# When the next pair's operands are given to the planner, and the order of GpSimd's sums

## The chip, the cores and the metric

The kernel runs on one core of a Trainium2 chip. The metric is device time in microseconds (us); less is better. The program is a single launch with float32 inputs and outputs.

## The reference

One layer of a decoder trunk for 1024 positions of width 1024: a token mixer (a gated delta rule beside a Conformer convolution), a cross-attention into 256 memory tokens, and a gated MLP with a short convolution between its two projections. Only the MLP's first half matters here:

```python
def conv_glu_ffn(h, w_up, conv_w, conv_b, w_down):     # h 1024 x 1024, w_up 1024 x 5632
    u = causal_dwconv(h @ w_up, conv_w) + conv_b       # width 3
    a, b = jnp.split(u, 2, axis=-1)
    return (jax.nn.silu(a) * b) @ w_down               # w_down 2816 x 1024
```

## The kernel before, in words

The 5632 columns of `w_up` are 44 blocks of 128. Block j of the first 22 and block j + 22 belong together (one is the gate, the other what it gates), so the up projection goes by pairs, j = 0 to 21. Pairs 0 and 1 are plain products. From `PLAIN` = 2 on, a pair is done by `strassen_pair` with seven half products instead of eight: the two weight blocks, each cut into two halves of K = 512, make the 2 x 2 operands A11, A12 (block j) and A21, A22 (block j + 22); the activations, cut by K and by position, make B11 to B22 and four combinations T1 to T4, which are made once ahead of the pairs.

`up_operands(j)` (L1171 to 1191) makes a pair's weights. It loads the two blocks on SyncE's queue (L1175; tile `raw_up`, two buffers in all), has GpSimd form S1 = A21 + A22, S2 = S1 - A11, S3 = A11 - A21 and S4 = A12 - S2 (L1183), and splits A11, S2, S1, S3, A12, S4 and A22 each into a rounded high part (ScalarE, L1188) and the rest (VectorE, L1189). The splits go into four slots of the tag `w`: (A11, S2), (S1, S3), (A12, S4) and (A22). A slot is free for the next pair when the previous pair's products from it are done. One buffer of `raw_up` is free when everything that reads it is done, the last of which is the split of A22 for the second block.

A half product is 12 matmuls (`mm3`, L242 to 244: high by high, high by low, low by high, for four slices of K) into one PSUM bank of 128 x 512. The order in `strassen_pair` is: A11 B11 into bank 0, S2 T2 into bank 1, S1 T1 into bank 2, S3 T3 into bank 3, then A12 B21 on top of bank 0, S4 B22 on top of bank 2, A22 T4 on top of bank 3. Before the last three, the first results must have been read out: L1204 (ScalarE) copies bank 0 to `p1`, L1206 (VectorE) adds bank 1 to it, L1208 makes `u3` = bank 2 + `p1`, L1210 makes a part of `ub` = bank 3 + `u3`. L1212, L1214 and L1216 read the final banks. Then `conv3` (L1157 ScalarE, L1159 VectorE twice for each block) and `gate_mid` (L1164 ScalarE, L1165 VectorE, store on ScalarE's queue, L1166) finish the pair beside the next pair's products.

What order the engines' queues have is not written out by hand: the Tile framework's planner goes through the program with a cost model of its own, and of what it takes as ready on an engine it puts first what the program gave it first. Every engine then works its queue in that fixed order and waits by semaphores. Before the change `up_operands(j + 1)` is called ahead of `strassen_pair(j)`, so all of the next pair's loads, sums and splits rank ahead of all of pair j's own work. `tc.keep_in_program_order(ins)` pins an instruction behind the one that the program gave the same engine before it; that is an order in the queue and no wait.

After the pairs the down projection (`down_operands`, `step_mm`) follows, with loads of `w_down` (`rbM`) and of the stored results (`ma`).

Of the kernel before, what the change touches and what calls it, by code (L numbers as in the profile page):

```python
# [7 lines left out]
F32 = mybir.dt.float32  # L8
# [8 lines left out]
P = 128  # L17
T = 1024
# [5 lines left out]
NFF = 22  # L24
# [45 lines left out]
def hybrid_layer(  # L70
# [4 lines left out]
    nc = tc.nc  # L75
# [41 lines left out]
    def set_psum(**tags):  # L117
        psum_es[0].close()
        psum_es[0] = ExitStack()
        psum_pool[0] = (psum_es[0].enter_context(pool("ps", space=PSUM)), tags)  # L120

    def psum(tag, name):
        p, tags = psum_pool[0]
        return p.tile([P, 512], F32, tag=tag, name=name, bufs=tags[tag])
# [18 lines left out]
    def raw_tile(shape, name):  # L143
        return wpool.tile(list(shape), F32, tag="raw", name=f"raw_{name}", bufs=2)
# [37 lines left out]
    for kind, i in in_order:  # L182
        j = col[kind] + i
# [57 lines left out]
    def mm3(o, wh, wl, xh, xl, start, stop, onto=False):  # L241
        pe.matmul(o, lhsT=wh, rhs=xh, start=start, stop=False, skip_group_check=onto)  # L242
        pe.matmul(o, lhsT=wh, rhs=xl, start=False, stop=False, skip_group_check=onto)  # L243
        pe.matmul(o, lhsT=wl, rhs=xh, start=False, stop=stop, skip_group_check=onto)  # L244
# [747 lines left out]
    def a_tile(shape, name, dtype=F32R):  # L992
        return ap_.tile(shape, dtype, tag="a", name=name, bufs=9)
# [124 lines left out]
    for t in range(NC):  # L1118
# [22 lines left out]
        s = slice((t % 4) * P, (t % 4 + 1) * P)  # L1141
# [12 lines left out]
    def conv3(j, ua):  # L1154
        u, a = ua[:, 0], ua[:, 1]
        fw = lambda n: par[:, O_FW + 3 * j + n:O_FW + 3 * j + n + 1]
        act.activation(a, u, AF.Identity, scale=fw(2), bias=par[:, O_FB + j:O_FB + j + 1])  # L1157
        for d in range(1, 3):
            dve.scalar_tensor_tensor(out=a[:, d:], in0=u[:, :T - d], scalar=fw(2 - d), in1=a[:, d:],  # L1159
                                     op0=ALU.mult, op1=ALU.add)  # L1160
        return a

    def gate_mid(j, a, b):
        act.activation(a, a, AF.Silu)  # L1164
        dve.tensor_tensor(a, a, b, op=ALU.mult)  # L1165
        nc.scalar.dma_start(out=mid_d[j], in_=a)  # L1166
# [4 lines left out]
    def up_operands(j):  # L1171
        r = []
        for jj in (j, j + NFF):
            raw = raw_tile((P, D), f"up{jj}")
            sync.dma_start(out=raw, in_=w_up[jj])  # L1175
            r.append(raw)
        op = {"A11": r[0][:, HS[0]], "A12": r[0][:, HS[1]], "A21": r[1][:, HS[0]], "A22": r[1][:, HS[1]]}
        sm = [tp.tile([P, 2, 512], F32, tag="tmp", name=f"sums{j}_{n}", bufs=2) for n in range(2)]
        for n, (s, p, m, alu) in enumerate((("S1", "A21", "A22", ALU.add), ("S2", "S1", "A11", ALU.subtract),
                                            ("S3", "A11", "A21", ALU.subtract),  # L1180
                                            ("S4", "A12", "S2", ALU.subtract))):
            op[s] = sm[n // 2][:, n % 2]
            nc.gpsimd.tensor_tensor(op[s], op[p], op[m], op=alu)  # L1183
        res = {}
        for n, names in enumerate(WOPS):
            w = wpool.tile([P, len(names), 2, 512], F32R, tag="w", name=f"wst{j}_{n}", bufs=4)
            for i, s in enumerate(names):
                act.activation(w[:, i, 0], op[s], AF.Copy)  # L1188
                dve.tensor_tensor(w[:, i, 1], op[s], w[:, i, 0], op=ALU.subtract)  # L1189
                res[s] = (w[:, i, 0], w[:, i, 1])  # L1190
        return res

    def half_product(o, w, xx, start):

        for k in range(4):
            c = slice(k * P, (k + 1) * P)
            mm3(o, w[0][:, c], w[1][:, c], xx[0][:, k], xx[1][:, k], start and k == 0, k == 3, not start)

    def strassen_pair(j, W_, ua, ub, tags="bbbb"):
        b = [psum({"m": "mm"}.get(tag, tag), f"st{j}_{n}") for n, tag in enumerate(tags)]  # L1200
        p1 = wpool.tile([P, 512], F32, tag="st", name=f"p{j}", bufs=2)
        u3 = gbp.tile([P, 512], F32, tag="gb", name=f"u3_{j}", bufs=1)
        half_product(b[0], W_["A11"], X["B11"], True)
        act.activation(p1, b[0], AF.Copy)  # L1204
        half_product(b[1], W_["S2"], X["T2"], True)
        dve.tensor_tensor(p1, b[1], p1, op=ALU.add)  # L1206
        half_product(b[2], W_["S1"], X["T1"], True)
        dve.tensor_tensor(u3, b[2], p1, op=ALU.add)  # L1208
        half_product(b[3], W_["S3"], X["T3"], True)
        dve.tensor_tensor(ub[:, 0, HS[1]], b[3], u3, op=ALU.add)  # L1210
        half_product(b[0], W_["A12"], X["B21"], False)
        act.activation(ua[:, 0, HS[0]], b[0], AF.Copy)  # L1212
        half_product(b[2], W_["S4"], X["B22"], False)
        dve.tensor_tensor(ua[:, 0, HS[1]], b[2], p1, op=ALU.add)  # L1214
        half_product(b[3], W_["A22"], X["T4"], False)
        dve.tensor_tensor(ub[:, 0, HS[0]], b[3], p1, op=ALU.add)  # L1216
        a = conv3(j, ua)
        gate_mid(j, a, conv3(j + NFF, ub))
# [48 lines left out]
    x_combination(3)  # L1267
    plain_out(1)
    ops = {PLAIN: up_operands(PLAIN)}
    for j in range(PLAIN, NFF):  # L1270
        if j + 1 < NFF:
            ops[j + 1] = up_operands(j + 1)
        strassen_pair(j, ops.pop(j), a_tile([P, 2, T], f"ua{j}", F32),
                      a_tile([P, 2, T], f"ua{j + NFF}", F32) if j % 2 else
                      tp.tile([P, 2, T], F32, tag="ua", name=f"ua{j + NFF}", bufs=1),
                      "gggm" if j == PLAIN else "bbbb")
        if j == PLAIN:
            set_psum(b=8)
# [230 lines left out]
```

## Time and profile before

| | us |
|---|---|
| median of 3 runs | 1477.58 (1476.55 to 1480.96) |
| the profiled execution | 1476.86, span 1474.9 |
| TensorE matmuls busy | 1426.9 (97%) |
| VectorE busy | 1163.1 (79%) |
| ScalarE busy | 694.9 (47%) |
| GpSimd busy | 151.8 (10%) |

The profiled execution is one run; the numbers below are of it. A matmul counts as busy from its issue to its modelled end, and neighbours overlap, so TensorE's speed is read from the distance between starts. In the profile PE is TensorE, PEld its weight loads, DVE VectorE, ACT ScalarE, POOL GpSimd, SPq SyncE's queue. The name `wst` is a split weight of a pair, `sums` are S1 to S4, `u` is `u3`, `st` a PSUM bank of a pair, `p` is `p1`. A name `x` as matmul operand is one of B11 to B22, `xT` one of T1 to T4, which tells the products apart.

### The profile page before, as it was taken

The page shows a single profiled execution, that of the slowest core. Times are in us where ns is not written, and L with a number is a line of the kernel's source. Part 1 is how long each engine was busy: PE and PEld are TensorE (multiplying, and loading weights), DVE is VectorE, ACT ScalarE, POOL GpSimd, SP SyncE. Part 2 cuts the span into 40 slices and gives each one's busy share as a digit, 9 for nine tenths or more (in the row PEclk, how much of TensorE's full clock was granted, in tenths as well). Part 3 has the DMA queues.
Part 4 walks back from the last instruction along what each step waited for, and adds up shares of the span by engine and source line. Part 5 has one row for each costly group of instructions (what it writes and reads, how often), then busy time and mean ns, then how long its engine had stood idle before and what let it go on. Part 6 is the DMA issues. An engine that isn't in the chain of part 4 may idle for free.

```text
span 1474.9 us, 19398 instructions
## 1 busy us (share of the span) xinstructions
PE 1426.9 (97%) x7087; PEld 1183.8 (80%) x7087; DVE 1163.1 (79%) x1971; ACT 694.9 (47%) x1309; POOL 151.8 (10%) x102
## 2 busy tenths in 40 slices
PE   6999999999999999999999999999999998999996
PEld 6878888888898878878888888888888886888875
DVE  6699999993567778743567988888888887779997
ACT  6526463642566545432534554444444444554442
POOL 0000000000000000000001233333333330000000
PEclk9999999999999999999999999999999999999998
DMA  7533232428756765310424532222222226985473
GB/s 249 165 97 93 80 101 77 123 96 273 240 170 202 244 221 188 129 70 1 157 101 143 171 100 72 86 86 86 73 75 82 86 86 202 341 291 189 142 252 110
DMA packets 121631, 212.01 MB, mean 144 GB/s; under 512 B 17440, under 2 KB 61120, under 8 KB 121536
## 3 DMA queue, kind: packets, MB, share of 16 engines
q1 hardware_dynamic: 97600, 159.13, 34.5%
q10 hardware_dynamic: 22976, 48.51, 8.8%
q0 software_dynamic: 960, 3.15, 0.7%
q8 instruction: 55, 0.90, 0.3%
q14 instruction: 40, 0.33, 0.1%
HBM read 156.73 MB, written 54.02 MB: 143 GB/s over the span
## 4 chain that ended last, share of the span: by engine, by line
PE 63%; DMA 12%; DVE 8%; POOL 7%; issue 5%; ACT 5%; SPq 0%; POOLq 0%; DVEq 0%; ACTq 0%
POOL sums L1183 7%; PE pj L244 6%; PE pj L242 6%; PE pj L243 6%; DMA raw_up<-in_w_up 4%; PE M L243 4%; PE M L244 4%; PE M L242 3%; PE st L242 3%; PE st L244 2%; PE st L243 2%; PE y L242 2%; PE y L243 2%; PE y L244 2%; PE sc L242 2%
## 5 line engine op out<-in xcount | busy, mean ns | idle before, releaser
L244 PE MATMUL pj<-xT,w_in 128*128 128x512 f32 x384 | 150.3, 391 | 1.2 <-DVE w_in L137 1.2
L242 PE MATMUL pj<-xT,w_in 128*128 128x512 f32 x384 | 150.8, 393 | 0.1
L358 DVE SCALAR_TENSOR_TENSOR ca<-sg,par,ca 128x1023 f32<-128x1023 f32 (+18 forms) x120 | 149.9, 1264 | 1.1
L243 PE MATMUL pj<-xT,w_in 128*128 128x512 f32 x384 | 149.9, 390 | 0.0
L243 PE MATMUL M<-wM 128*128 128x512 f32 x308 | 121.5, 395 | 4.2 <-DVE wM L1343 2.7
L242 PE MATMUL st<-xT,wst 128*128 128x512 f32 x320 | 124.5, 389 | 0.0
L243 PE MATMUL st<-xT,wst 128*128 128x512 f32 x320 | 124.5, 389 | 0.0
L244 PE MATMUL st<-xT,wst 128*128 128x512 f32 x320 | 124.5, 389 | 0.0
L242 PE MATMUL M<-wM 128*128 128x512 f32 x308 | 119.6, 395 | 5.0 <-ACT wM L136 3.4
L244 PE MATMUL M<-wM 128*128 128x512 f32 x308 | 121.0, 393 | 0.0
L1159 DVE SCALAR_TENSOR_TENSOR ua<-ua,par 128x1023 f32<-128x1023 f32 x88 | 112.5, 1280 | 10.3 <-ACT ua L1157 7.3
L242 PE MATMUL st<-x,wst 128*128 128x512 f32 x240 | 95.6, 398 | 1.8
L243 PE MATMUL st<-x,wst 128*128 128x512 f32 x240 | 93.7, 391 | 0.0
L244 PE MATMUL st<-x,wst 128*128 128x512 f32 x240 | 93.5, 390 | 0.0
L136 ACT ACTIVATE wM<-rbM 128x1024 fp32r<-128x1024 f32 x55 | 58.0, 1062 | 74.8 <-PE M L244 48.6
L1189 DVE TENSOR_TENSOR wst<-sums,wst 128x512 fp32r<-128x512 f32 x80 | 63.5, 815 | 34.5 <-ACT wst L1188 34.5
L1188 ACT ACTIVATE wst<-sums 128x512 fp32r<-128x512 f32 x80 | 46.0, 620 | 93.8 <-POOL sums L1183 93.8
L244 PEld LDWEIGHTS pj<-xT,w_in 128*128 128x128 f32 x384 | 72.1, 188 | 16.1 <-DVE w_in L137 1.4
L242 PEld LDWEIGHTS pj<-xT,w_in 128*128 128x128 f32 x384 | 72.1, 188 | 14.9 <-ACT w_in L136 0.3
L243 PEld LDWEIGHTS pj<-xT,w_in 128*128 128x128 f32 x384 | 72.2, 188 | 14.5
L137 DVE TENSOR_TENSOR wM<-rbM,wM 128x1024 fp32r<-128x1024 f32 x55 | 66.6, 1218 | 8.8 <-ACT wM L136 8.8
L243 PEld LDWEIGHTS M<-wM 128*128 128x128 f32 x308 | 58.5, 190 | 18.3 <-DVE wM L1343 3.6
(383 smaller groups left out, 3568.5 us busy)
## 6 DMA issues: line engine op xcount, KB each, us to landing
rbM<-in_w_down SPq DMA_DIRECT2D x132, 256.0 KB, 3.9
raw_up<-in_w_up SPq DMA_DIRECT2D x44, 512.0 KB, 3.6
raw_in<-in_w_in SPq DMA_DIRECT2D x24, 512.0 KB, 3.7
mid_d<-ua ACTq DMA_DIRECT2D x22, 512.0 KB, 2.6
ma<-mid_d SPq DMA_DIRECT2D x44, 256.0 KB, 5.3
raw_kv<-in_w_kv SPq DMA_DIRECT2D x16, 512.0 KB, 3.7
h_d<-h ACTq DMA_DIRECT2D x16, 512.0 KB, 2.7
xr<-in_x ACTq DMA_DIRECT2D x8, 512.0 KB, 5.4
```

Of the source, the lines that this page charges most:

```text
L136: act.activation(w[:, 0], raw, AF.Copy)
L137: dve.tensor_tensor(w[:, 1], raw, w[:, 0], op=ALU.subtract)
L242: pe.matmul(o, lhsT=wh, rhs=xh, start=start, stop=False, skip_group_check=onto)
L243: pe.matmul(o, lhsT=wh, rhs=xl, start=False, stop=False, skip_group_check=onto)
L244: pe.matmul(o, lhsT=wl, rhs=xh, start=False, stop=stop, skip_group_check=onto)
L358: dve.scalar_tensor_tensor(out=ca[:, d:], in0=sg[:, :T - d], scalar=par[:, wb + 30 - d:wb + 31 - d], in1=ca[:, d:], op0=ALU.mult, op1=ALU.add)
L1159: dve.scalar_tensor_tensor(out=a[:, d:], in0=u[:, :T - d], scalar=fw(2 - d), in1=a[:, d:], op0=ALU.mult, op1=ALU.add)
L1183: nc.gpsimd.tensor_tensor(op[s], op[p], op[m], op=alu)
L1188: act.activation(w[:, i, 0], op[s], AF.Copy)
L1189: dve.tensor_tensor(w[:, i, 1], op[s], w[:, i, 0], op=ALU.subtract)
```

## The change

The call of `up_operands(j + 1)` moves from ahead of `strassen_pair(j)` into it, behind L1208 (`u3`), and `strassen_pair` takes its operands from `ops` itself. GpSimd's four sums are each pinned in the order of the program: S1, S2, S3, S4.

```diff
             op[s] = sm[n // 2][:, n % 2]
-            nc.gpsimd.tensor_tensor(op[s], op[p], op[m], op=alu)
+            tc.keep_in_program_order(nc.gpsimd.tensor_tensor(op[s], op[p], op[m], op=alu))
...
-    def strassen_pair(j, W_, ua, ub, tags="bbbb"):
+    def strassen_pair(j, ua, ub, tags="bbbb"):
+        W_ = ops.pop(j)
...
         dve.tensor_tensor(u3, b[2], p1, op=ALU.add)
+        if j + 1 < NFF:
+            ops[j + 1] = up_operands(j + 1)
         half_product(b[3], W_["S3"], X["T3"], True)
...
     for j in range(PLAIN, NFF):
-        if j + 1 < NFF:
-            ops[j + 1] = up_operands(j + 1)
-        strassen_pair(j, ops.pop(j), a_tile([P, 2, T], f"ua{j}", F32),
+        strassen_pair(j, a_tile([P, 2, T], f"ua{j}", F32),
```

## Rows read from the trace of the kernel before

**Rows 1.** Busy time by stretch: span, busy (count) of each engine, PEclk, DMA share, GB/s

```profile
872.00:1222.00 350.00, 348.18 (x1513) 282.15 (x1512) 286.20 (x306) 153.10 (x216) 128.72 (x72) 1.00 0.25 82
1241.00:1474.00 233.00, 215.50 (x927) 174.72 (x925) 203.06 (x307) 107.44 (x158) 0.00 (x0) 0.98 0.67 227
```

**Rows 2.** Waits from 853 to 1241 us: who waited for whom, total us, times, longest

```profile
ACT wst L1188 <- POOL sums L1183: 93.8, 19, 6.6
...
PEld st L242 <- DVE u L1208: 9.4, 18, 0.5
```

**Rows 3.** The chain of waits in one pair: start us, us, what

```profile
951.53 3.56 DMA raw_up<-in_w_up
955.25 5.87 POOL sums L1183 x3
961.14 0.64 ACT wst L1188
```

**Rows 4.** TensorE's timeline: first matmuls of pairs 2, 3 and 21, last of 21

```profile
853.05 0.39 PE L242 MATMUL st<-x,wst 128*128 128x512 f32 x1
...
872.09 0.39 PE L242 MATMUL st<-x,wst 128*128 128x512 f32 x1
...
1222.37 0.39 PE L242 MATMUL st<-x,wst 128*128 128x512 f32 x1
...
1241.19 0.39 PE L244 MATMUL st<-xT,wst 128*128 128x512 f32 x1
```

**Rows 5.** TensorE's timeline in one pair: third product's last matmul, sixth, seventh product

```profile
957.75 0.39 PE L244 MATMUL st<-xT,wst 128*128 128x512 f32 x1
...
963.19 0.39 PE L244 MATMUL st<-x,wst 128*128 128x512 f32 x1
963.68 0.50 PE L242 MATMUL st<-x,wst 128*128 128x512 f32 x1
...
966.53 0.39 PE L242 MATMUL st<-xT,wst 128*128 128x512 f32 x1
```

**Rows 6.** VectorE's timeline in the same pair

```profile
956.54 1.72 DVE L1165 TENSOR_TENSOR ua<-ua,ua 128x1024 f32<-128x1024 f32 x1
958.18 1.77 DVE L1189 TENSOR_TENSOR wst<-raw_up,wst 128x512 fp32r<-128x512 f32 x1
961.80 1.22 DVE L1189 TENSOR_TENSOR wst<-sums,wst 128x512 fp32r<-128x512 f32 x1 [1.84 <-ACT wst L1188]
962.95 0.68 DVE L1208 TENSOR_TENSOR u<-st,p 128x512 f32<-128x512 f32 x1
963.73 0.69 DVE L1210 TENSOR_TENSOR ua<-st,u 128x512 f32<-128x512 f32 x1
964.34 1.28 DVE L1189 TENSOR_TENSOR wst<-sums,wst 128x512 fp32r<-128x512 f32 x2
```

**Rows 7.** GpSimd's timeline in the same pair

```profile
955.24 1.94 POOL L1183 TENSOR_TENSOR sums<-raw_up 128x512 f32<-128x512 f32 x1 [12.21 <-DMA raw_up<-in_w_up]
957.14 2.27 POOL L1183 TENSOR_TENSOR sums<-raw_up,raw_up 128x512 f32<-128x512 f32 x1
959.37 1.73 POOL L1183 TENSOR_TENSOR sums<-sums,raw_up 128x512 f32<-128x512 f32 x1
961.18 1.30 POOL L1183 TENSOR_TENSOR sums<-raw_up,sums 128x512 f32<-128x512 f32 x1
```

**Rows 8.** ScalarE's timeline in the same pair

```profile
961.67 1.14 ACT L1188 ACTIVATE wst<-sums 128x512 fp32r<-128x512 f32 x2
...
966.73 0.63 ACT L1188 ACTIVATE wst<-raw_up 128x512 fp32r<-128x512 f32 x1 [2.52 <-PE st L244]
```

**Rows 9.** VectorE's timeline in pair 2

```profile
863.10 0.69 DVE L1208 TENSOR_TENSOR u<-st,p 128x512 f32<-128x512 f32 x1
866.74 1.22 DVE L1189 TENSOR_TENSOR wst<-sums,wst 128x512 fp32r<-128x512 f32 x1 [2.95 <-ACT wst L1188]
```

**Rows 10.** L1183's instructions, the one for S2: duration ns min/median/max

```profile
L1183 POOL TENSOR_TENSOR sums<-sums,raw_up x20: 1279/1732/1751, 831.6 to 1212.5; 128x512 f32<-128x512 f32 x20
```

## The prediction

> **What bounds the kernel now.** I began with the page's busy times, in the table above: TensorE has matmuls in flight 97% of the span, so only time in which TensorE stands still, or work taken off it, can move the end. The change touches the up projection's pairs alone (j = 2 to 21), so next came the busy times by stretch [rows 1]: from 872 to 1222 us TensorE is idle 1.8 of 350 us at granted clock 1.00, VectorE has 64 us free, GpSimd works a third of the time, DMA a quarter. Nothing there is near a limit except TensorE.
>
> The waits of the stretch [rows 2] name one stall of TensorE: in 18 pairs the weight load of L242 waits for VectorE's L1208 (u3 = bank 2 + p1). The other long waits (ScalarE 93.8 us for GpSimd's sums) are of engines that are not the bound, but the chain of waits shows that they feed this stall [rows 3]: load of the second weight block, three sums on GpSimd, ScalarE's split of S2, VectorE's split of S2, u3, TensorE.
>
> TensorE's own starts give the price [rows 4]. Pair 2 runs from 853.05 to 872.09, 19.04 us; pair 21 from 1222.37 to 1241.19 + 0.23, 19.05. These two have no such stall. 84 matmuls in 19.04 us are 0.2267 us each. Pairs 3 to 20 take (1222.37 - 872.09) / 18 = 19.460 us each. So a pair loses 0.415 us, and 18 pairs 350.28 - 18 x 19.045 = **7.5 us**. That is all that the change can win in its stage.
>
> One pair in detail (TensorE [rows 5], VectorE [rows 6], GpSimd [rows 7], ScalarE [rows 8]): bank 2 is complete at 957.75 + 0.39 = 958.14. VectorE does L1206, the gate L1165 until 958.26, the low half of the next pair's A11 until 959.95, then stands 1.84 us in front of the low half of the next pair's S2, which ScalarE can give only when GpSimd has summed S2 (third, ends 961.10). u3 stands behind it in VectorE's queue and ends at 963.63; TensorE, due at 963.19 + 0.23 = 963.42 with the sixth product, which writes bank 2 again, starts at 963.68.
>
> **The change part by part.**
>
> *The place of the operands.* What up_operands(j+1) issues (2 loads on SyncE, 4 sums on GpSimd, 7 splits on ScalarE and 7 on VectorE) now ranks behind pair j's first three products, L1204, L1206 and L1208, instead of ahead of them. No instruction is added or taken away. On SyncE the loads are passed by nothing, since a pair puts nothing else there; its store goes out by ScalarE's queue behind the gate, as before. On ScalarE L1204 already runs ahead of the next pair's splits. On VectorE u3 comes ahead of S2's split, and probably of A11's: ready at 958.14, with VectorE free at 958.26, it would end about 958.9, 4.4 us ahead of need. A11's split then ends 0.7 us later, about 960.6, and is not due before the next pair's first product, 3 x 2.7 us later. If u3 were put even ahead of L1165, VectorE would stand up to 958.14 - 956.54 = 1.6 us with L1165 and the splits queued behind; it has (350 - 286.2) / 18 = 3.5 us free per pair [rows 1], so that also costs nothing. Pair 2 shows the wanted order already: u3 at 863.10, S2's split at 866.74 [rows 9], and that pair has no stall.
>
> *GpSimd's order.* Today it is S1, S3, S2, S4; pinned it is S1, S2, S3, S4. The pin is an order on GpSimd's own queue and adds no wait for another engine. S2 reads S1, so it pays the gap that S4 pays behind S2: 961.18 - 961.10 = 0.08 us. S2's duration at its new place, beside L1165 and A11's split, is not in the trace. Bounds: 1.28 (its shortest [rows 10]) and 2.27 (S3, which stands in that place now); I take 1.73, its median. S1 ends at 957.18, so S2 ends at 958.99 (958.5 to 959.5), 2.1 us earlier than now.
>
> *If u3 still stood behind S2's split*, this alone would do: ScalarE 959.03 to 959.66; VectorE from 959.95 when A11's split is done, 1.22 us as now or 1.77 beside a sum, so 961.2 to 961.7; u3 0.68 more, 961.9 to 962.4 (with S2 at 2.27: 962.7). TensorE needs it by about 963.37. Margin 0.7 to 1.5 us. Either edit removes the stall; both together cannot remove it twice.
>
> *What is late next.* S3 moves to third place and ends about 961.3. ScalarE splits S1 and S3 from 961.67 today, when their weight slot is free, so this costs nothing up to 0.4 us, and beyond that has cover: they are for the next pair. S4 ends with the same four durations, about 962.5, and is split at about 967.3, when the sixth product has given its slot back (the ScalarE row of 966.73 waits for TensorE). The next bank readout, L1210, frees bank 3 for the seventh product at 966.53 [rows 5]. It stays behind the operands in rank. At worst it comes behind the splits of S1 and S3 (1.28 us together, today from 964.34): ScalarE ends 962.8, VectorE about 964.2, L1210 964.9, 1.6 us ahead of need. The second weight block's split at a pair's start ranks as now against the previous pair's tail, so the loads go out when they do now, counted from a pair's start.
>
> *Behind the stage.* Pair 21 has no next operands and no stall, so it keeps its 19.05 us. The down projection is idle on TensorE 233 - 215.5 = 17.5 us [rows 1]; its loads are released by the last pairs' work and move forward with it. The planner lays out the whole program anew, though, and the order there may shift. Cost taken as 0, bounds from the nearest row: a third of those 17.5 us either way, about 6.
>
> **The sum.** The profiled execution took 1476.86 us (span 1474.9); less 7.5 is 1469.4. The median of the three runs stands 0.7 higher, and less 7.5 is 1470.1. I say **1469.7**, 0.5% faster.
>
> **The rivals.**
>
> *The stall is a shortage of buffers, not of order.* For it: S2 is late because the second weight block's load goes out only at 951.53, when its buffer is free, and the same gap comes 18 times. Against it: u3 needs bank 2 and p1 alone, and both are there 4.8 us before it runs; in pair 2 S2's split came 3.6 us behind u3 [rows 9], and there was no stall. If it held, nothing would change: 1476.9. The Trainium skill ("Perfetto Trace Analysis", section "Optimization Strategy") says that a gap that repeats on the engine that should be full can mean too few buffers for the next tile. By that rule the time would be that of this rival; the trace agrees for GpSimd's wait of 12.21 us for the load [rows 7], and not for TensorE's.
>
> *The planner sets u3 further back.* It works with its own durations, and today it took S2's split to be ready before u3. Should it also put the splits of S1 and S3 ahead, u3 would end about 963.1 + 0.7 = 963.8 instead of 963.63: 0.17 us more in 18 pairs, 1479.9, still within what can't be told from no change. Against it: those splits wait for the slot that the fourth product frees, 2.7 us after bank 2 is complete.
>
> *The stall moves to bank 3 (slower).* L1210 ranks behind all of the next pair's operands. If VectorE's queue had it behind the splits of A12 and S4, which wait for the sixth product's end (ScalarE from 966.73, VectorE until 968.7), it would end at 969.4, and the seventh product would start 2.9 us late: 19 x 2.9 = 55 us, less 7.5, 1524. It decides once L1210 ends later than 966.5, 2.1 us later than today's 964.42. Against it: it ranks behind them today too and runs ahead.
>
> *The gain is taken back in the down projection* by another order: 6 us give 1475.7; more than 12, which is two thirds of all the idle time there, would be needed for slower.
>
> **How the numbers follow.** A measurement of this kernel can tell a change of about 0.3%, 4.4 us. Forecast 0.80, its own range 1467.5 to 1472.5. Buffers 0.04, u3 further back 0.05, bank 3 0.03, a loss in the down projection 0.08, of which 0.05 ends within 0.3% and 0.03 slower. So faster 0.80, same 0.14, slower 0.06. The range goes from 1466.5 (3 us won behind the stage) to 1476.5, just under the unchanged time, and leaves out under 2 in 10.
>
> **What would show it.** Right: pairs 3 to 20 at 19.0 to 19.1 us between their first matmuls; the row of TensorE waiting for L1208 gone; on VectorE u3 ahead of S2's split, or behind it but done before the sixth product; on GpSimd the sum that reads sums and raw_up second; the down projection's 233 us unchanged. Wrong: pairs at 19.46 with u3 behind a split (rival one or two), a wait of TensorE for L1210, or pairs at 19.05 and a longer down projection.

## The result

The changed kernel takes 1470.13 us in the median of 5 runs (1467.92 to 1472.68), the kernel before 1479.33 in 5 runs of its own (1476.55 to 1481.84): ratio 0.9936, 95% interval 0.9919 to 0.9954. In a second comparison, beside the experiments below, it was 0.9944 (0.9927 to 0.9961). It is faster by about half a per cent, as forecast (1469.7, range 1466.5 to 1476.5). The medians lie 9.2 us apart here and 7.0 in the second comparison (1477.01 and 1469.97). Single runs of one kernel differ by some 5 us, so the time alone can't tell where the gain comes from; the traces below do. The profiled execution has a span of 1468.3 us against 1474.9.

In the changed kernel L1205, L1207 and L1209 (`u3`) answer to L1204, L1206 and L1208 of before, and L1213 (bank 3's readout) to L1210.

**The profile after.** The shares of the chain of waits by engine; GpSimd, with 7% in the chain of before, is gone from it:

```profile
PE 83%; DMA 7%; DVE 6%; issue 2%; ACT 2%; SPq 0%; DVEq 0%; ACTq 0%
```

Busy times in the stretch of the first of [rows 1], in the same columns. TensorE has 350.00 us of 350 now, where it had 348.18:

```profile
872.00:1222.00 350.00, 350.00 (x1545) 289.49 (x1544) 298.27 (x316) 160.33 (x223) 134.34 (x72) 1.00 0.26 85
```

The waits from 853 to 1241 us, to set beside [rows 2]. ScalarE waits 30 us less for the sums, and TensorE's 18 waits for `u3` have become one:

```profile
ACT wst L1188 <- POOL sums L1183: 63.6, 18, 6.5
...
PEld st L242 <- DVE u L1209: 0.4, 1, 0.4
```

TensorE's starts, to set beside [rows 4]: first matmuls of pairs 2, 3, 4 and 21 and the last of pair 21.

```profile
855.32 0.39 PE L242 MATMUL st<-x,wst 128*128 128x512 f32 x1
...
874.36 0.39 PE L242 MATMUL st<-x,wst 128*128 128x512 f32 x1
...
893.69 0.39 PE L242 MATMUL st<-x,wst 128*128 128x512 f32 x1
...
1217.37 0.39 PE L242 MATMUL st<-x,wst 128*128 128x512 f32 x1
...
1236.18 0.39 PE L244 MATMUL st<-xT,wst 128*128 128x512 f32 x1
```

Pair 2 takes 19.04 us, pair 3 still 19.33, pairs 4 to 20 (1217.37 - 893.69) / 17 = 19.04. From pair 2's first matmul to 0.23 behind the last one it is 381.09 us; before it was 1241.19 + 0.23 - 853.05 = 388.37 [rows 4]. The stage gave 7.28 us. The two spans differ by only 6.6 us, because the stage began 2.27 us later in this execution and what came behind it took 1.6 us less; in the profiles below neither has a pattern by kernel.

The same stretch of a pair (it starts at 950.81; that of [rows 6] at 949.81) on VectorE, to set beside [rows 6]:

```profile
957.54 1.72 DVE L1165 TENSOR_TENSOR ua<-ua,ua 128x1024 f32<-128x1024 f32 x1
959.18 1.77 DVE L1189 TENSOR_TENSOR wst<-raw_up,wst 128x512 fp32r<-128x512 f32 x1
960.88 0.68 DVE L1209 TENSOR_TENSOR u<-st,p 128x512 f32<-128x512 f32 x1
961.48 1.18 DVE L1189 TENSOR_TENSOR wst<-sums,wst 128x512 fp32r<-128x512 f32 x1
962.59 0.68 DVE L1213 TENSOR_TENSOR ua<-st,u 128x512 f32<-128x512 f32 x1
963.19 1.78 DVE L1189 TENSOR_TENSOR wst<-sums,wst 128x512 fp32r<-128x512 f32 x2
```

and on GpSimd, to set beside [rows 7]: S1, S2 (the one that reads sums and raw_up), S3, S4.

```profile
956.32 1.86 POOL L1183 TENSOR_TENSOR sums<-raw_up 128x512 f32<-128x512 f32 x1 [11.54 <-DMA raw_up<-in_w_up]
958.26 2.15 POOL L1183 TENSOR_TENSOR sums<-sums,raw_up 128x512 f32<-128x512 f32 x1
960.37 1.75 POOL L1183 TENSOR_TENSOR sums<-raw_up,raw_up 128x512 f32<-128x512 f32 x1
962.08 1.74 POOL L1183 TENSOR_TENSOR sums<-raw_up,sums 128x512 f32<-128x512 f32 x1
```

`u3` has changed places with S2's split and ends at 961.56, 10.75 us behind the pair's start. The sixth product starts without a break:

```profile
964.18 0.39 PE L244 MATMUL st<-x,wst 128*128 128x512 f32 x1
964.41 0.39 PE L242 MATMUL st<-x,wst 128*128 128x512 f32 x1
```

so there are 2.85 us to spare. On VectorE's whole queue the two kernels differ in 18 exchanges of neighbours and nothing else: `u3` with S2's split in pairs 4 to 20, and L1207 with A11's split in pair 2. In pair 3 the planner left `u3` behind S2's split, and that pair kept its stall.

### The profile page after: what moved, and what is told of

It reads as the page before. It is cut to its first block, busy times and chain, and to the rows that moved or that the text cites. A ratio compares the mean times of both kernels' runs of the same rounds, so it can differ in the third digit from the quotient of the medians.

```text
span 1468.3 us, 19399 instructions
## 1 busy us (share of the span) xinstructions
PE 1422.7 (97%) x7087; PEld 1186.8 (81%) x7087; DVE 1168.4 (80%) x1971; ACT 696.7 (47%) x1309; POOL 157.2 (11%) x102
## 4 chain that ended last, share of the span: by engine, by line
PE 83%; DMA 7%; DVE 6%; issue 2%; ACT 2%; SPq 0%; DVEq 0%; ACTq 0%
PE st L244 8%; PE st L242 8%; PE st L243 8%; PE pj L244 6%; PE pj L242 6%; PE pj L243 6%; PE M L243 4%; PE M L244 4%; PE M L242 3%; PE y L243 2%; PE y L242 2%; PE y L244 2%; PE sc L242 2%; PE sc L243 2%; PE sc L244 2%
## 5 line engine op out<-in xcount | busy, mean ns | idle before, releaser
L1159 DVE SCALAR_TENSOR_TENSOR ua<-ua,par 128x1023 f32<-128x1023 f32 x88 | 112.5, 1281 | 10.2 <-ACT ua L1157 7.2
L1189 DVE TENSOR_TENSOR wst<-sums,wst 128x512 fp32r<-128x512 f32 x80 | 71.8, 918 | 3.0 <-ACT wst L1188 3.0
```

## The experiments

Theory 1: `u3` stood behind work in VectorE's queue that it does not need; whatever brings `u3`, or the work ahead of it, in time takes the stall away. Theory 2: the late load of the second weight block (two buffers) sets the pair, whatever the order. Theory 3: only the place of the operands counts. Theory 4: only the order of GpSimd's sums counts.

Lengths of the pairs in all profiles in us, from TensorE's starts (for pairs 4 to 20 the mean), with the time from the stage's end to the span's end:

```
kernel                    pair 2  pair 3  pairs 4-20  stage   start of pair 2  behind the stage
before                    19.04   19.33   19.47       388.4   853.1            233.5
changed                   19.04   19.33   19.04       381.1   855.3            231.9
the pin alone             19.04   19.33   19.04       381.1   854.7            232.2
the move alone            19.97   19.75   19.04       382.5   856.7            234.3
changed, once more        19.04   19.69   19.04       381.5   853.1            233.7
u3 first                  19.04   19.04   19.04       380.8   850.4            233.1
late load, u3 ahead       20.76   20.89   19.04       384.4   855.2            234.0
late load, u3 behind      26.23   19.77   19.74       400.7   856.1            232.4
late load, no pin         19.04   24.85   19.04       386.6   852.3            234.9
```

**The pin alone.**

```diff
-            nc.gpsimd.tensor_tensor(op[s], op[p], op[m], op=alu)
+            tc.keep_in_program_order(nc.gpsimd.tensor_tensor(op[s], op[p], op[m], op=alu))
```

> GpSimd's sums in the order S1, S2, S3, S4, but the operands given ahead of the pair as before, so that u3 stays behind the split of S2 in VectorE's queue. Theory 1 (u3 stands behind work that it doesn't need, and either edit alone brings it in time): S2's sum ends about 1.6 us earlier than before, u3 ends about 12.1 us behind a pair's start instead of 13.8 and is due at 13.6; pairs 4 to 20 take 19.04 us, the time is that of the changed kernel, about 1470. Theory 2 (the late load of the second block, a shortage of buffers, sets the stall): the pairs stay at 19.46, 1479. Theory 3 (only the place of the operands counts): the same, 1479.

Measured: 1471.15 us (12 runs), ratio to before 0.9963 (0.9948 to 0.9978). VectorE's whole queue stands in the order of before; what is new is GpSimd's order alone. VectorE in the pair that starts at 950.21: S2's split is still ahead of `u3` (L1208 here), but now in time:

```profile
960.51 1.55 DVE L1189 TENSOR_TENSOR wst<-sums,wst 128x512 fp32r<-128x512 f32 x1 [0.15 <-ACT wst L1188]
961.98 0.68 DVE L1208 TENSOR_TENSOR u<-st,p 128x512 f32<-128x512 f32 x1
```

The wait of 1.84 us in front of the split [rows 6] is 0.15, `u3` ends 12.45 us behind the start, 1.15 ahead of need, and pairs 4 to 20 are 19.04. The sums start as late as before (5.3 to 5.6 us behind the start of pairs 4 to 20 in both profiles), so theory 2 falls; the operands are given where they were before, so theory 3 falls too.

**The move alone.** The diff of the change without its first hunk.

> The operands given behind u3, but GpSimd's order left free (S1, S3, S2, S4), so that S2 comes as late as before. Theory 1: u3 stands ahead of S2's split in pairs 4 to 20 and ends about 10.8 us behind a pair's start; pairs of 19.04 us, about 1470; S2's split then makes VectorE wait some 2 us a pair, which costs nothing. Theory 2: 19.46 and 1479, as S2 and the loads are as late as before. Theory 4 (only GpSimd's order counts): 1479.

Measured: 1471.41 us (6 runs), ratio 0.9949 (0.9930 to 0.9968). VectorE in the pair that starts at 953.58: `u3`, the wait, S2's split, bank 3's readout.

```profile
963.65 0.68 DVE L1209 TENSOR_TENSOR u<-st,p 128x512 f32<-128x512 f32 x1
965.57 1.22 DVE L1189 TENSOR_TENSOR wst<-sums,wst 128x512 fp32r<-128x512 f32 x1 [1.25 <-ACT wst L1188]
966.72 0.68 DVE L1213 TENSOR_TENSOR ua<-st,u 128x512 f32<-128x512 f32 x1
```

`u3` ends 10.75 us behind the start, the split waits 1.25 us for ScalarE, and TensorE doesn't feel it. Theory 4 falls: either edit is enough for pairs 4 to 20, and together they give no more there. Without the pin the readout of bank 3 ends 13.82 us behind the start, with it 12.45 (due 16.3). In pair 2 of this execution, where the sums began only 10.2 us behind the start, it was too late and TensorE waited for it:

```profile
PEld st L242 <- DVE ua L1213: 1.0, 1, 1.0
```

The seventh product of that pair started 0.8 us late. In the second profile of the changed kernel (next run) pair 2's sums began later still, 10.4 us behind the start, and with S2 summed second the readout ended in time, at 15.5. That speaks for the pin there, by one pair of one execution each; pair 3 kept its stall for `u3` here too (0.6 us).

**The changed kernel again.**

> The changed kernel once more, for a second profile beside the others. The stage's gain should stand again: pairs 4 to 20 at 19.04 us, pair 3 at 19.33. What is not order should scatter: the up projection's start (853.05 before, 855.32 after the change, with the same order ahead of it) and the time from its end to the end of the span (233.5 and 231.9). Theory 1 says that these two are spread of single executions and not the change: across these four profiles they vary by 1 to 2 us without a pattern by kernel. Rival: the 1.6 us behind the stage are the change's, and stand in every kernel with it.

Measured: 1469.97 us (6 runs), ratio 0.9944 (0.9927 to 0.9961). The stage gained again (381.5), with pair 3 at 19.69 instead of 19.33. The table's last two columns scatter over 6.4 and 3.0 us with no pattern by kernel: behind the stage, of the five profiles with one edit or both and the ordinary load, two lie above the 233.5 of before and three below. The 1.6 us gained behind the stage in the first profile were scatter of single executions and not the change's.

**u3 first in every pair.** `tc.issue_after(i)` puts what is given inside it behind `i` where both are on the same engine's queue; it orders the queue and adds no work.

```diff
-        dve.tensor_tensor(u3, b[2], p1, op=ALU.add)
+        i3 = dve.tensor_tensor(u3, b[2], p1, op=ALU.add)
         if j + 1 < NFF:
-            ops[j + 1] = up_operands(j + 1)
+            with tc.issue_after(i3.ins):
+                ops[j + 1] = up_operands(j + 1)
```

> As the changed kernel, with the next pair's work on each pair's VectorE queue put behind u3 by an edge of order, so that u3 comes ahead of the splits of A11 and of S2 in all pairs, pair 3 too. Theory 1: u3 ends about 9.2 us behind a pair's start, 4.4 us ahead of need; pairs 4 to 20 stay at 19.04 (no more is to be had), pair 3 loses its 0.29 us stall: 0.3 us less than the changed kernel, not to be told apart in the time. If u3 or its margin still cost something in pairs 4 to 20, they would fall below 19.04.

Measured: 1469.95 us (6 runs), ratio 0.9941 (0.9923 to 0.9958), not to be told from the changed kernel. Pair 3 on VectorE, first of the changed kernel (the pair starts at 874.36) and then of this one (869.39):

```profile
885.68 1.78 DVE L1189 TENSOR_TENSOR wst<-sums,wst 128x512 fp32r<-128x512 f32 x1
887.39 0.68 DVE L1209 TENSOR_TENSOR u<-st,p 128x512 f32<-128x512 f32 x1
```

```profile
877.76 0.68 DVE L1207 TENSOR_TENSOR p<-st,p 128x512 f32<-128x512 f32 x1
878.54 0.69 DVE L1209 TENSOR_TENSOR u<-st,p 128x512 f32<-128x512 f32 x1
879.15 1.64 DVE L1189 TENSOR_TENSOR wst<-raw_up,wst 128x512 fp32r<-128x512 f32 x1
880.71 1.78 DVE L1189 TENSOR_TENSOR wst<-sums,wst 128x512 fp32r<-128x512 f32 x1
```

All 20 pairs are 19.04, 380.8 us together: no pair has a stall left.

**A late load, u3 ahead.** The changed kernel, and in `up_operands`:

```diff
             sync.dma_start(out=raw, in_=w_up[jj])
+            if jj >= NFF:
+                sync.dma_start(out=raw, in_=w_up[jj])
```

> The changed kernel with the second weight block loaded twice into the same buffer, one load behind the other, so that S1, S2, S3 and S4 come about 3.7 us later in every pair; u3 stays ahead of S2's split and bank 3's readout stays behind it. Theory 1 (order in VectorE's queue): u3 doesn't move; S2's split ends about 15.2 us behind a pair's start instead of 11.9, bank 3's readout about 15.9, due at 16.3: pairs stay at 19.04 us, 1470, with 0.4 us to spare. Theory 2 (the late load itself sets the pair): 3.3 us more in each of 18 pairs, about 1530.

Measured: 1474.76 us (10 runs), ratio to before 0.9978 (0.9963 to 0.9994). Pairs 4 to 20 stay at 19.04 with the sums 3.4 us later behind a pair's start (8.9 instead of 5.5), which theory 2 cannot give. In the pair that starts at 954.0, GpSimd's S1 and then VectorE:

```profile
962.87 1.28 POOL L1185 TENSOR_TENSOR sums<-raw_up 128x512 f32<-128x512 f32 x1 [13.35 <-DMA raw_up<-in_w_up]
```

```profile
960.73 1.22 DVE L1165 TENSOR_TENSOR ua<-ua,ua 128x1024 f32<-128x1024 f32 x1
961.86 0.68 DVE L1191 TENSOR_TENSOR wst<-raw_up,wst 128x512 fp32r<-128x512 f32 x1
962.46 0.68 DVE L1211 TENSOR_TENSOR u<-st,p 128x512 f32<-128x512 f32 x1
966.21 1.11 DVE L1191 TENSOR_TENSOR wst<-sums,wst 128x512 fp32r<-128x512 f32 x1 [3.07 <-ACT wst L1190]
967.24 0.68 DVE L1215 TENSOR_TENSOR ua<-st,u 128x512 f32<-128x512 f32 x1
```

Bank 3's readout ends 13.9 us behind the start and not at the 15.9 expected, since the sums are shorter here (below). What the stage lost against the changed kernel is in pairs 2 and 3, 3.3 us, where the sums begin later still (12.8 and 9.9 us behind the pair's start): TensorE waited once for bank 3's readout (pair 2) and once for `u3`, which is behind S2's split in pair 3. That was not in the expectation.

**A late load, u3 behind S2's split.** The same double load with the pin, the operands in their old place, and `u3` put behind VectorE's split of the next pair's S2, which `s2_low` keeps:

```diff
-                dve.tensor_tensor(w[:, i, 1], op[s], w[:, i, 0], op=ALU.subtract)
+                low = dve.tensor_tensor(w[:, i, 1], op[s], w[:, i, 0], op=ALU.subtract)
+                if s == "S2":
+                    s2_low[j] = low.ins
...
-        dve.tensor_tensor(u3, b[2], p1, op=ALU.add)
+        with tc.issue_after(s2_low.get(j + 1, s2_low[j])):
+            dve.tensor_tensor(u3, b[2], p1, op=ALU.add)
```

> The same late second load and the same pinned sums, but the operands given ahead of the pair and u3 put behind the next pair's S2 split on VectorE by an edge of order. Theory 1: u3 ends about 15.6 us behind a pair's start instead of the 13.6 at which it is due, so the sixth product starts 2.0 to 2.4 us late in 18 pairs: pairs of about 21.2 us and 1510. Theory 2: the same as the run with u3 ahead, about 1530 in both. If u3's place didn't matter at all: 1470.

Measured: 1488.15 us (4 runs), ratio 1.0070 (1.0052 to 1.0089). TensorE waits for `u3` (L1213 here) in 19 pairs:

```profile
PEld st L242 <- DVE u L1213: 19.4, 19, 4.6
```

The direction and the place are those of theory 1: the same load costs nothing in pairs 4 to 20 with `u3` ahead and 0.70 us a pair with `u3` behind. In those pairs the VectorE queues of the two kernels differ by this one exchange and nothing else. The size is a third of the 2.2 us expected, mainly since the sums got shorter where they now fall: S1 and S2 together by 1.5 us. GpSimd's groups for S2, in the changed kernel from 893 to 1217 us and in this one from 902 to 1237:

```profile
L1183 POOL TENSOR_TENSOR sums<-sums,raw_up 128x512 f32<-128x512 f32 x17 | 36.6, 2155 | 1.3
```

```profile
L1185 POOL TENSOR_TENSOR sums<-sums,raw_up 128x512 f32<-128x512 f32 x17 | 21.9, 1288 | 1.3
```

**A late load without the pin.** The kernel of the late load with `u3` ahead, less the pin.

> The same late second load with the operands given behind u3, but GpSimd's order left free, so that S2 is summed third. u3 is ahead of S2's split, bank 3's readout behind it. Theory 1 with its second half (what the pin is worth: it keeps bank 3's readout, which stays behind S2's split, ahead of the seventh product): S2's split ends about 17.1 us behind a pair's start, the readout 17.8, due at 16.3: the seventh product starts 1.5 us late, pairs of about 20.5 us, 1497, and TensorE's wait is for the readout of bank 3 and not for u3. Without that half (the pin is worth nothing once u3 is ahead): 19.04 and 1470. Theory 2: about 1530.

Measured: 1477.47 us (10 runs), ratio 0.9991 (0.9979 to 1.0003). The expectation of a stall at bank 3 failed: pairs 4 to 20 are 19.04, and TensorE never waits for bank 3. In the pair that starts at 953.35 the readout ends 15.2 us behind the start instead of 17.8, again mainly because the three sums up to S2 take 1.29 us each and not 1.7 to 2.3:

```profile
966.75 1.22 DVE L1191 TENSOR_TENSOR wst<-sums,wst 128x512 fp32r<-128x512 f32 x1 [4.25 <-ACT wst L1190]
967.89 0.68 DVE L1215 TENSOR_TENSOR ua<-st,u 128x512 f32<-128x512 f32 x1
```

What the stage lost is in pair 3, with one stall of 4.1 us for `u3`. What the pin is worth beside the move is thus shown only in margin (1.37 us for bank 3), and in pair 2 of the run without it.

No run gave `raw_up` a third buffer. By theory 1 an earlier load would bring S2's split in time as well; the runs show that it isn't needed, not that it wouldn't help.

## Why the prediction was right

*The bound and the price of the stall.* Right. The price from pairs with and without the stall, 7.5 us, came out as 7.28 in the trace, 17 pairs of 0.43 us. The eighteenth is pair 3, where the planner kept `u3` behind S2's split and the stall of 0.29 us stayed: 19.33 us is outside the 19.0 to 19.1 that the prediction named for pairs 3 to 20, and one wait for `u3` is left. The prediction took the order of all 18 pairs from one of them. That the median came within 0.4 us of the forecast is partly luck: the medians of before lie between 1477.0 and 1479.3 in the three comparisons.

*Where u3 would stand.* Ahead of S2's split: right, but for pair 3. Ahead of A11's split ("probably"): wrong; A11's stayed first, `u3` ended 10.75 us behind a pair's start and not 9.1. The margin was 2.85 us instead of 4.4, so it changed nothing, and the run with `u3` first in every pair shows that the place ahead of A11 is worth nothing in pairs 4 to 20.

*GpSimd's order.* The gap of S2 behind S1 was 958.26 - 958.18 = 0.08 us, as taken. S2's duration was 2.15, near the upper bound of 2.27 and not the median of 1.73 that was taken: in the second place it lies beside L1165 and A11's split. Where the late load moves it past those two it takes 1.29 us, L1165 then 1.22 instead of 1.72 and A11's split 0.68 instead of 1.77, while `u3`, with one input in PSUM, takes 0.68 with a sum beside it (18 pairs of the changed kernel) and without. The Trainium skill ("SBUF — State Buffer", section "Who interferes with whom") says that a VectorE instruction with two SBUF inputs contends with a GpSimd instruction that reads SBUF. These durations agree.

*That either edit suffices.* Right for pairs 4 to 20, by the two runs with one edit each. Behind S2's split `u3` had 1.15 us to spare, within the 0.7 to 1.5 worked out.

*What is late next.* Right: bank 3's readout ended 3.85 us ahead of need. The planner put it ahead of the splits of S1 and S3, so the worst case of 1.6 did not come. One reading was off without harm: before the change the split of S1 and S3 at 961.67 [rows 8] came right behind ScalarE's split of S2 and did not wait for its slot; in the changed kernel it starts 0.8 us earlier in its pair, and there the slot is what it waits for.

*Behind the stage.* Right in kind: 233.5 us before, 231.9 to 234.3 in five profiles with one edit or both at the ordinary load. The 6 us held open either way were too wide; no order changed there on VectorE.

*The rivals.* The shortage of buffers was wrong for TensorE: with the load later still, pairs 4 to 20 kept 19.04 us. The Trainium skill as cited there ("Perfetto Trace Analysis", section "Optimization Strategy") says that such a repeated gap can mean too few buffers. The traces don't agree here: the gap went with the same two buffers, by the order of a queue. The other rivals did not come about, though bank 3's readout did stop TensorE in pair 2 of two runs: 0.8 us with the move alone, and 1.6 us with the late load and `u3` ahead.

## What to carry to other kernels

Where the bound engine waits for one short instruction, look at what stands ahead of that instruction in its own engine's queue, and whether it needs it. Price the stall by the distance between the starts of equal pieces of work with it and without it: the row of waits told 9.4 us for 18 stalls that cost 7.5, and 4.6 us for a long one that cost 7.2. A planner's order for one piece of a loop need not be that of the others: the first ones, where the loop fills, keep their own stalls.

## What the runs showed of the hardware

A long stall costs more than its wait. In the run with the late load and `u3` behind, TensorE stood in pair 2 from the matmul of 869.43 to 873.96, and its starts were 0.43 us apart afterwards:

```profile
869.43 0.39 PE L244 MATMUL st<-x,wst 128*128 128x512 f32 x1
873.96 0.79 PE L242 MATMUL st<-x,wst 128*128 128x512 f32 x1 [4.14 <-DVE u L1213]
874.55 0.63 PE L243 MATMUL st<-x,wst 128*128 128x512 f32 x1
874.98 0.63 PE L244 MATMUL st<-x,wst 128*128 128x512 f32 x1
```

The busy times ahead of it and behind it give the granted clock (the column behind the engines) as 1.00 and then 0.50, the lower of the two levels, 1.2 GHz:

```profile
860.00:869.00 9.00, 9.00 (x42) 7.44 (x41) 5.36 (x6) 2.07 (x3) 0.09 (x1) 1.00 0.61 165
874.00:879.60 5.60, 5.60 (x13) 4.41 (x14) 2.30 (x4) 0.11 (x1) 0.44 (x1) 0.50 0.00 0
```

Pair 2 took 26.23 us, 7.2 more than its 19.04, for a distance between starts that was 4.3 us too long; from 880 us the clock is 1.00 again. The run with the late load and no pin shows it a second time: in pair 3 TensorE stood from the matmul of 884.75 to 889.20, the clock is 0.50 from 889.2 to 892.2 and 1.00 from 893, and the pair took 5.8 us more for a distance that was 4.2 too long. The stalls of 0.3 us of the kernel before, and those of 1.6 to 1.7 us in pairs 2 and 3 of the run with `u3` ahead, left the clock at 1.00 in the stretches behind them.
